# A decoder trunk on one core: the first four recurrent tiles with the tokens as the stationary side, turned by transfers, and the first gating batch behind another order of units

## The chip, the cores and the metric

One core of one Trainium2 chip runs the whole kernel. The metric is device time of one execution in microseconds. Three runs of the kernel before gave 965.71, 966.05 and 967.69, a median of 966.05 us. Beside these stands one profiled execution with its trace; every row quoted below is from it.

## The reference

A trunk of two layers over 256 tokens of width 1024, in float32. Layer 0 mixes tokens by a gated linear recurrence (RG-LRU), layer 1 by attention; around each mixer stand two half-step SwiGLU networks of width 2816, and every part is normalised before and after. The change touches the recurrent block only:

```python
def recurrent_block(x, w_in, conv_w, conv_b, w_a, b_a, w_x, b_x, lam, w_out):
    gx = x @ w_in
    gate, rec = gx[..., :D_RNN], gx[..., D_RNN:]
    rec = causal_depthwise_conv(rec, conv_w, conv_b)
    rec = rg_lru(rec, w_a, b_a, w_x, b_x, lam)
    return (jax.nn.gelu(gate) * rec) @ w_out
```

D_RNN is 1344. The convolution has four taps along the tokens. Inside rg_lru two small block-diagonal products (16 blocks of 84) with a sigmoid give the gates r and i; then log_a = -8 r softplus(-lam), a = exp(log_a), u = sqrt(1 - a^2) i x, and the state is h = a h + u along the tokens.

## The kernel before, in words

**Products.** Every operand is cut into a high and a low half: on the weights' side ACT copies the high half (whi, line 173) and DVE subtracts the low half (wlo, line 177). A product is three matmuls: high by high, low by high, high by low. `mm3` (lines 181 to 185) holds tokens still and streams weight columns; `mm3w` (lines 187 to 192) holds weights still and streams the 256 tokens.

**Units.** The program is a list of items, each with a `prep` (load on SP's queue into one of 5 raw buffers, then the split into one of 9 pairs of buffers) and a `work` (matmuls). `slot` runs one item for one half of the tokens (t = 0 or 1) or for both, then calls `tick`. `tick` counts down deferred steps (`defer(n, fn)` runs fn n ticks later), starts the next item's prep, and takes steps from a queue, each with a price, against a purse of 0.8 a tick. The order of TensorE's instructions is as written; ACT, DVE, POOL and SP are ordered by the framework, by when each step becomes possible and by what waits for it.

**The recurrent stage.** Its 1344 recurrent columns are eleven tiles of rows: ten of 126 and one of 84, in pairs p = 0 to 5. Units g0 to g10 make the gate branch, tokens still (g0 to g3 the first 504 columns, g4 to g7 the next 504, g8 to g10 the last 336; "0g5" is unit 5 for t = 0). Units r0 to r5 make the recurrent branch, weights still, so that the result has channels on the partitions and tokens along the row: 96 matmuls of 256 tokens for r0 and r1 together. `RG_ORDER` is the order of units, written by hand.

**From a pair to y.** After r_p, `conv` (lines 741 to 759) copies the pair out of its bank on ACT (line 748) and adds three taps a tile on DVE (line 754). Unit gw_p (line 761) multiplies it by the gate blocks into two banks (line 795), and ACT takes tanh of these (line 809). `after_gates` then has tanh and exp on ACT (line 828) and a chain on DVE (lines 829 to 838). For every two pairs stands a `batch` (line 845): a square root on ACT (line 853), the pending gelus of the gate branch (line 856), on DVE the products and the scan (lines 861, 862, 867), the gate branch turned by TensorE (line 877) or, for t = 0 of batches 0 and 1, by a transfer (`gate_turn`, line 694: POOL copies to 16-bit halves, an SP transfer transposes, POOL joins), the product y (line 886), its high half on ACT (line 887) and its low half on DVE (line 892). tanh, exp, square root and gelu need table loads on ACT where they follow one another. `w_out` (lines 183 to 185, reading y) takes tile k of y as its step k: steps 0 to 3 are batch 0, 4 to 7 batch 1, 8 to 10 batch 2. For t = 0 it runs eight steps, then six for t = 1, then the rest.

Of the kernel before, what the change touches and what calls it, by code (L numbers as in the profile page):

```python
# [43 lines left out]
def trunk_kernel(ctx: ExitStack, tc: tile.TileContext, A: dict, out: bass.AP):  # L44
# [13 lines left out]
    def nm(s):  # L58
        uid[0] += 1
        return f"{s}_{uid[0]}"  # L60
# [20 lines left out]
    def defer(n, fn):  # L81
        pend.append([n, fn])
# [73 lines left out]
    def load_raw(src, parts, n, pieces=1):  # L156
        v = new_raw()[:parts, :n]
        if len(src.shape) == 3:
            a, m = src.shape[1] // pieces, n // pieces
            for c in range(pieces):  # L160
                nc.sync.dma_start(v[:, c * m:(c + 1) * m].rearrange("p (a b) -> p a b", a=a),
                                  src[:, c * a:(c + 1) * a, :])
        else:
            nc.sync.dma_start(v, src)
        return v
# [52 lines left out]
    def join(dst, turned):  # L218

        nc.gpsimd.tensor_copy(dst, turned.rearrange("p (h f) -> p h f", h=2))  # L220
# [436 lines left out]
    def w_in(c0, n, k0, kn):  # L657
        return A["rg_w_in"][0, k0 * P:(k0 + kn) * P, c0:c0 + n].rearrange("(k p) n -> p k n", p=P)
# [6 lines left out]
    def add_gate_unit(g, k0, kn):  # L665
        c0, nn = GCOLS[g]

        def prep():
            return split(load_raw(w_in(c0, nn, k0, kn), P, kn * nn), P, kn * nn)

        def work(t, u):
            if k0 == 0:
                gacc[(g, t)] = mmbank()
            ps = gacc[(g, t)][:, :nn]
            for j in range(kn):
                k = k0 + j
                mm3(ps, *main_x(t, k), u.hi[:, j * nn:(j + 1) * nn], u.lo[:, j * nn:(j + 1) * nn], k == 0, k == 7)
            if k0 + kn == 8:

                if t not in toks:  # L680
                    toks[t] = pools["r"].tile([P, DRNN], F32, name=f"tok{t}")
                tok = toks[t][:, c0:c0 + nn]
                if t == 0 and g < 2:
                    nc.scalar.activation(tok, ps, AF.Gelu_apprx_tanh)
                    defer(5 - 3 * g, lambda: gate_turn(g))
                else:
                    nc.scalar.activation(tok, ps, AF.Copy)
                    plain.append(tok)
        rg[f"g{sum(n[0] == 'g' and n[1] != 'w' for n in rg)}"] = len(items)
        items.append((prep, work))  # L690
# [3 lines left out]
    def gate_turn(g):  # L694

        halves = hpool.tile([P, 512], F32, tag="t1", name=nm("pl"), bufs=2).bitcast(U16)
        hv = halves.rearrange("p (h j f) -> p h j f", h=2, j=4)
        src = toks[0][:, 4 * g * RT:4 * (g + 1) * RT].bitcast(U16)
        nc.gpsimd.memset(hv[:, :, :, RT:], 0)
        nc.gpsimd.tensor_copy(hv[:, :, :, :RT], src.rearrange("p (j f h) -> p h j f", h=2, f=RT))  # L700
        turned = pools["r"].tile([P, 512], F32, tag="turned", name=nm("turned"), bufs=1).bitcast(U16)
        out = tokT[g] = pools["r"].tile([P, 4, P], F32, tag="tokT", name=nm("tokT"), bufs=2)
        flat = out.rearrange("p a b -> p (a b)").bitcast(U16).rearrange("p (f h) -> p h f", h=2)
        defer(1, lambda: swap(turned, halves))
        defer(4, lambda: join(flat, turned))

    def tiles_of(p):
        return [2 * p, 2 * p + 1] if p < 5 else [10]
# [32 lines left out]
    def conv(p, ps):  # L741
        tl, w = tiles_of(p), pw(p)
        if p >= 4:
            flush(("y", (p - 4) // 2))
        xc = pools["r"].tile([RT, 2, S], F32, tag="xc", name=nm("xc"), bufs=4)
        xcs[p] = xc
        for j, i in enumerate(tl):
            nc.scalar.activation(xc[:w, j, :], ps[:w, j * S:(j + 1) * S], AF.Identity,
                                 bias=par[:w, 4 * NRT + i:4 * NRT + i + 1], scale=par[:w, 3 * NRT + i:3 * NRT + i + 1])

        def taps(j, i):
            for k in (2, 1, 0):
                s = 3 - k
                nc.vector.scalar_tensor_tensor(xc[:w, j, s:], ps[:w, j * S:(j + 1) * S - s],
                                               par[:w, k * NRT + i:k * NRT + i + 1], xc[:w, j, s:], ALU.mult, ALU.add)

        first = [(1.25, ("c", p), lambda j=j, i=i: taps(j, i)) for j, i in enumerate(tl)]
        n = max([i for i, q in enumerate(queue) if q[1][0] == "c"], default=-1)
        queue[n + 1:n + 1] = first
# [147 lines left out]
    def parts_of(g):  # L907
        return [(0, 4, RT)] if g < 2 else [(0, 2, RT), (2, 3, BLK)]

    for g in range(2):  # L910
        for k0 in range(0, 8, 2):
            add_gate_unit(g, k0, 2)
    for p in range(4):
        add_rec_units(p)
    for k0 in (0, 3, 6):
        add_gate_unit(2, k0, min(3, 8 - k0))
    add_rec_units(4)
# [1 line left out]
    for p in range(6):  # L919
        gw_unit(p)  # L920
    n_rg = len(items)
    RG_ORDER = ("0g0 0g1 0g2 0g3 0g4 0g5 0g6 0g7 1g0 1g1 r0 1g2 r1 gw0 1g3 1g4 r2 gw1 1g5 1g6 r3 gw2 1g7 "
                "0g8 0g9 0g10 r4 gw3 r5 1g8 gw4 1g9 1g10 gw5").split()
    OUT_ORDER = [0] * 8 + [1] * 6 + [0] * 3 + [1] * 5

    gbox = {}
# [543 lines left out]
```

## Time and profile before

| What | Value |
|---|---|
| median of 3 runs | 966.05 us |
| the profiled execution | 965.92 us |
| its span, first to last instruction | 964.2 us |
| outside the span | 1.7 us |
| granted TensorE clock over the span | 0.999 |
| TensorE busy | 955.9 us |
| DVE busy | 640.7 us |
| ACT busy | 527.6 us |
| POOL busy | 218.2 us |
| recurrent stage on TensorE, from first gate unit to w_out | about 190 to 268 us |

The profile is a page and a trace that answers questions: a timeline of one engine (start, length, engine, line, operation, tiles and shapes, how many were put together, and in brackets idle time before with its releaser), the chain of work that ended last, the waits by line, groups of equal instructions, and busy times by stretches. All times count from the start of the span. In a timeline, a row's length is that of the instruction with its latency; the next one on the engine can start before its end, so a run of instructions is added up from start to start.

### The profile page before, as it was taken

The page shows a single profiled execution, that of the slowest core. Times are in us where ns is not written, and L with a number is a line of the kernel's source. Part 1 is how long each engine was busy: PE and PEld are TensorE (multiplying, and loading weights), DVE is VectorE, ACT ScalarE, POOL GpSimd, SP SyncE. Part 2 cuts the span into 40 slices and gives each one's busy share as a digit, 9 for nine tenths or more (in the row PEclk, how much of TensorE's full clock was granted, in tenths as well). Part 3 has the DMA queues.
Part 4 walks back from the last instruction along what each step waited for, and adds up shares of the span by engine and source line. Part 5 has one row for each costly group of instructions (what it writes and reads, how often), then busy time and mean ns, then how long its engine had stood idle before and what let it go on. Part 6 is the DMA issues. An engine that isn't in the chain of part 4 may idle for free.

```text
span 964.2 us, 12866 instructions
## 1 busy us (share of the span) xinstructions
PE 955.9 (99%) x4575; PEld 791.3 (82%) x4575; DVE 640.7 (66%) x845; ACT 527.6 (55%) x750; POOL 218.2 (23%) x221
## 2 busy tenths in 40 slices
PE   9999999999999999999999999999999999999997
PEld 6888888898878888888898888888887788888886
DVE  6658674678997666664686566665488876666642
ACT  7546453568886555443565455444366855444431
POOL 2712330130001323230003522234022012232200
PEclk9999999999999999999999999999999999999999
DMA  8787995475346787775558979878773468777731
GB/s 286 226 258 225 256 284 197 142 228 163 119 123 219 209 236 211 205 242 196 135 182 278 253 219 258 230 216 265 226 256 97 133 199 236 207 222 233 223 109 44
DMA packets 148934, 198.79 MB, mean 206 GB/s; under 512 B 67166, under 2 KB 85958, under 8 KB 148742
## 3 DMA queue, kind: packets, MB, share of 16 engines
q1 hardware_dynamic: 146182, 191.06, 65.6%
q0 software_dynamic: 2080, 6.38, 2.1%
q8 instruction: 36, 0.59, 0.2%
q10 hardware_dynamic: 608, 0.53, 0.2%
q14 instruction: 28, 0.23, 0.1%
HBM read 182.19 MB, written 3.16 MB: 192 GB/s over the span
## 4 chain that ended last, share of the span: by engine, by line
PE 95%; DVE 2%; ACT 1%; issue 1%; POOL 0%; DMA 0%; POOLq 0%; DVEq 0%; ACTq 0%
PE mm L428 16%; PE mm L429 16%; PE mm L432 16%; PE mm L183 13%; PE mm L185 13%; PE mm L184 13%; PE gt L795 2%; PE mm L1305 1%; PE mm L190 1%; PE mm L191 1%; PE mm L192 1%; PE gt L226 1%; ACT pe L1181 1%; DVE wlo L177 0%; PE tr L127 0%
## 5 line engine op out<-in xcount | busy, mean ns | idle before, releaser
L177 DVE TENSOR_TENSOR wlo<-raw,whi 128x1024 fp32r<-128x1024 f32 (+5 forms) x329 | 418.0, 1276 | 230.7 <-ACT whi L173 228.3
L173 ACT ACTIVATE whi<-raw 128x1024 fp32r<-128x1024 f32 (+5 forms) x329 | 341.9, 1045 | 308.6 <-PE mm L432 119.2
L428 PE MATMUL mm<-whi,xhi 128*128 128x512 f32 x656 | 256.6, 391 | 0.0
L429 PE MATMUL mm<-wlo,xhi 128*128 128x512 f32 x656 | 255.5, 389 | 0.0
L432 PE MATMUL mm<-whi,xlo 128*128 128x512 f32 x656 | 202.1, 389 | 0.0
L428 PEld LDWEIGHTS mm<-whi,xhi 128*128 128x128 f32 x656 | 123.2, 188 | 25.9 <-issue 0.7
L432 PEld LDWEIGHTS mm<-whi,xlo 128*128 128x128 f32 x656 | 123.1, 188 | 25.8 <-DVE xlo L240 0.2
L429 PEld LDWEIGHTS mm<-wlo,xhi 128*128 128x128 f32 x656 | 123.2, 188 | 25.4 <-DVE wlo L177 0.3
L183 PE MATMUL mm<-whi,hhi 128*128 128x512 f32 x352 | 137.2, 390 | 0.0
L185 PE MATMUL mm<-whi,hlo 128*128 128x512 f32 x352 | 137.0, 389 | 0.0
L184 PE MATMUL mm<-wlo,hhi 128*128 128x512 f32 x352 | 136.9, 389 | 0.0
L540 POOL COPY pl<-prod 128x1024 uint16<-128x1024 uint16 (+1 forms) x48 | 69.9, 1456 | 174.4 <-DMA prod<-pl 174.4
L527 POOL COPY pl<-prod 128x1024 uint16<-128x1024 uint16 (+1 forms) x48 | 66.3, 1382 | 151.9 <-DVE prod L524 86.8
L183 PEld LDWEIGHTS mm<-whi,hhi 128*128 128x128 f32 x352 | 66.1, 188 | 13.7
L185 PEld LDWEIGHTS mm<-whi,hlo 128*128 128x128 f32 x352 | 66.1, 188 | 13.7
L184 PEld LDWEIGHTS mm<-wlo,hhi 128*128 128x128 f32 x352 | 66.1, 188 | 13.6
L198 POOL TENSOR_SCALAR nv<-ss 128x1 f32<-128x1 f32 x22 | 9.6, 437 | 268.7 <-ACT junk L205 268.7
L524 DVE SCALAR_TENSOR_TENSOR prod<-mm,rstd,sil 128x512 f32<-128x512 f32 (+1 forms) x48 | 33.8, 703 | 29.5 <-PE mm L432 25.9
L515 ACT ACTIVATE sil<-mm,rstd 128x512 f32<-128x512 f32 (+1 forms) x48 | 31.0, 649 | 32.9 <-PE mm L432 25.0
L546 DVE TENSOR_TENSOR hlo<-pl,hhi 128x512 fp32r<-128x512 f32 (+1 forms) x48 | 41.2, 858 | 3.7 <-ACT hhi L545 3.7
L183 PE MATMUL mm<-whi,xhi 128*128 128x512 f32 (+1 forms) x112 | 42.8, 382 | 0.0
L185 PE MATMUL mm<-whi,xlo 128*128 128x512 f32 (+1 forms) x112 | 42.5, 379 | 0.0
(223 smaller groups left out, 1054.6 us busy)
## 6 DMA issues: line engine op xcount, KB each, us to landing
raw<-in_ffn_w_down_dram SPq DMA_DIRECT2D x88, 512.0 KB
raw<-in_ffn_w_up_dram SPq DMA_DIRECT2D x80, 512.0 KB
raw<-in_ffn_w_gate_dram SPq DMA_DIRECT2D x78, 512.0 KB
raw<-in_rg_w_in_dram SPq DMA_DIRECT2D x10, 504.0 KB
raw<-in_rg_w_out_dram SPq DMA_DIRECT2D x10, 504.0 KB
raw<-in_ffn_w_gate_dram SPq DMA_DIRECT2D x19, 256.0 KB
raw<-in_ffn_w_up_dram SPq DMA_DIRECT2D x16, 256.0 KB
raw<-in_rg_w_in_dram SPq DMA_DIRECT2D x8, 512.0 KB
```

The costliest lines, as they stand in the source:

```text
L173: up = nc.scalar.activation(hi[:parts, c:c + m], rawv[:, c:c + m], AF.Copy)
L177: nc.vector.tensor_tensor(lo[:parts, c:c + m], rawv[:, c:c + m], hi[:parts, c:c + m].bitcast(F32), ALU.subtract)
L183: nc.tensor.matmul(ps, xh, wh, start=first, stop=False)
L184: nc.tensor.matmul(ps, xh, wl, start=False, stop=False)
L185: nc.tensor.matmul(ps, xl, wh, start=False, stop=last)
L428: nc.tensor.matmul(ps, get_x(t, k)[0], u.hi[:, c], start=k == 0, stop=False)
L429: nc.tensor.matmul(ps, get_x(t, k)[0], u.lo[:, c], start=False, stop=False)
L432: nc.tensor.matmul(ps, get_x(t, k)[1], u.hi[:, c], start=False, stop=k == nk - 1)
L524: nc.vector.scalar_tensor_tensor(pr[:, :nn], ps, rs[t][:, 0:1], s, ALU.mult, ALU.mult)
L527: nc.gpsimd.tensor_copy(halves.rearrange("p (h f) -> p h f", h=2), pr[:, :nn].bitcast(U16).rearrange("p (f h) -> p h f", h=2))
L540: nc.gpsimd.tensor_copy(halves.rearrange("p (f h) -> p h f", h=2), turned.rearrange("p (h a) b -> p h (a b)", h=2))
L546: keep(nc.vector.tensor_tensor(lv, x, hv.bitcast(F32), ALU.subtract))
```

## The change

Three things change.

1. r0 and r1 go. In their place a new kind of unit, `add_tok_unit` (R0 to R3, for t = 0 and 1), multiplies the first 504 recurrent columns with the tokens still: 6 matmuls of 504 columns a unit, 48 in all. After R3 the result has tokens on the partitions. ACT copies it (rtok), POOL copies it to 16-bit halves, an SP transfer transposes it, and POOL joins the halves into rT. The convs of pairs 0 and 1 come 7 and 8 ticks after 1R3 and read rT; their ACT copies are pinned in the order of the program.
2. `RG_ORDER` is a new one. gw0 stands after 0g7 and 1g4 stands behind it; r2 and 1g3 now stand ahead of gw0. From gw1 on TensorE's order of units is as it was, but for 1g6, which stands behind gw2 and no longer ahead of r3.
3. `gate_turn(0)` is deferred by 9 ticks, not by 5.

The functions behind keep their text and move in the file: lines 746 to 784 of before are 37 further down, 785 to 959 are 40 further down.

The framework's order on the other engines shifts with it. Four places follow. The names in the rows are: th gates, tt the batch's work tile, xc a conv's pair, y the batch's result, tok a gate tile, whi and wlo halves of a weight.

ACT at the first batch's square root (the 126x1024 row). Before:

```order
L748 ACTIVATE xc_2147<-mm_2098,par 126x256 x2
L809 ACTIVATE th_2166<-gt_2153,hb 126x256
L809 ACTIVATE th_2167<-gt_2153,hb 126x256
L809 ACTIVATE th_2166<-gt_2154,hb 126x256
L809 ACTIVATE th_2167<-gt_2154,hb 126x256
L828 ACTIVATE tt_2075<-th_2166,sp_101 126x256 x2
L828 ACTIVATE th_2166<-th_2166,sp_102 126x256 x2
L173 ACTIVATE whi_2348<-raw_2346 128x1008
L173 ACTIVATE whi_2392<-raw_2390 128x672
L853 ACT_TABLE_LOAD
L853 ACTIVATE tt_2075<-tt_2075 126x1024
```

and now:

```order
L868 ACT_TABLE_LOAD
L868 ACTIVATE th_2123<-th_2123,sp_102 126x256 x2
L849 ACTIVATE th_2166<-gt_2153,hb 126x256
L849 ACTIVATE th_2166<-gt_2154,hb 126x256
L849 ACTIVATE th_2167<-gt_2153,hb 126x256
L849 ACTIVATE th_2167<-gt_2154,hb 126x256
L173 ACTIVATE whi_2182<-raw_2180 128x1008
L868 ACTIVATE tt_2147<-th_2166,sp_101 126x256 x2
L868 ACTIVATE th_2166<-th_2166,sp_102 126x256 x2
L173 ACTIVATE whi_2282<-raw_2280 128x672
L893 ACT_TABLE_LOAD
L893 ACTIVATE tt_2147<-tt_2147 126x1024
```

Before, two pairs of conv copies and three weight splits lay between pair 0's and pair 1's gates; now pair 0's exp stands right ahead of pair 1's gates.

ACT in w_out, from y of batch 1 to the square roots of batch 2. Before:

```order
L887 ACTIVATE y_2588<-y_2587 126x512
L887 ACTIVATE y_2588<-y_2592 126x512
L828 ACTIVATE th_2533<-th_2533,sp_102 126x256
L809 ACTIVATE th_2606<-gt_2597,hb 84x256
L809 ACTIVATE th_2607<-gt_2597,hb 84x256
L828 ACTIVATE tt_2600<-th_2606,sp_101 84x256
L173 ACTIVATE whi_2645<-raw_2643 126x1024
L828 ACTIVATE th_2606<-th_2606,sp_102 84x256
L173 ACTIVATE whi_2661<-raw_2659 126x1024
L853 ACT_TABLE_LOAD
L853 ACTIVATE tt_2600<-tt_2600 126x512
L853 ACTIVATE tt_2600<-tt_2600 84x256
```

and now, from the second y row on:

```order
L927 ACTIVATE y_2561<-y_2565 126x512
L868 ACTIVATE tt_2589<-th_2500,sp_101 126x256
L868 ACT_TABLE_LOAD
L868 ACTIVATE th_2500<-th_2500,sp_102 126x256 x2
L173 ACTIVATE whi_2621<-raw_2619 126x1024
L868 ACTIVATE tt_2589<-th_2579,sp_101 84x256
L893 ACT_TABLE_LOAD
L893 ACTIVATE tt_2589<-tt_2589 126x512
L868 ACT_TABLE_LOAD
L868 ACTIVATE th_2579<-th_2579,sp_102 84x256
L173 ACTIVATE whi_2680<-raw_2678 126x1024
L893 ACT_TABLE_LOAD
```

Before, both square roots of batch 2 follow one table load. Now pair 4's root comes ahead of the exp of pair 5 (84 rows), whose root follows after two more table loads.

DVE at the products of batch 1. Before:

```order
L867 SCALAR_TENSOR_TENSOR tt_2418<-th_2278,tt_2418 126x256 x2
L867 SCALAR_TENSOR_TENSOR tt_2418<-th_2458,tt_2418 126x256 x2
L829 SCALAR_TENSOR_TENSOR xc_2436<-th_2534,xc_2436 126x512
L886 TENSOR_TENSOR y_2587<-tokT_1906,tt_2418 126x512
L886 TENSOR_TENSOR y_2592<-tr_2582,tt_2418 126x512
L892 TENSOR_TENSOR y_2589<-y_2587,y_2588 126x512
L892 TENSOR_TENSOR y_2589<-y_2592,y_2588 126x512
L833 TENSOR_SCALAR th_2533<-th_2533 126x512
L834 SCALAR_TENSOR_TENSOR th_2534<-tt_2600,th_2533 126x512
```

and now:

```order
L869 SCALAR_TENSOR_TENSOR xc_2409<-th_2501,xc_2409 126x512
L907 SCALAR_TENSOR_TENSOR tt_2447<-th_2425,tt_2447 126x256 x2
L177 TENSOR_TENSOR wlo_2576<-raw_2573,whi_2575 126x1024
L926 TENSOR_TENSOR y_2560<-tokT_2133,tt_2447 126x512
L926 TENSOR_TENSOR y_2565<-tr_2555,tt_2447 126x512
L177 TENSOR_TENSOR wlo_2586<-raw_2583,whi_2585 126x1024
L932 TENSOR_TENSOR y_2562<-y_2560,y_2561 126x512
L932 TENSOR_TENSOR y_2562<-y_2565,y_2561 126x512
L869 SCALAR_TENSOR_TENSOR xc_2467<-th_2580,xc_2467 84x256
```

Now one weight split stands between the last scan and the first product, and one between the second product and the lows.

ACT where the first conv stands, now:

```order
L687 ACTIVATE tok_1983<-mm_1939 128x512
L173 ACTIVATE whi_1988<-raw_1986 128x960
L173 ACTIVATE whi_2012<-raw_2010 128x960
L785 ACTIVATE xc_2028<-rT_1829,par 126x256 x2
L785 ACTIVATE xc_2047<-rT_1829,par 126x256 x2
L785 ACTIVATE xc_2065<-mm_1997,par 126x256 x2
L173 ACTIVATE whi_2070<-raw_2068 128x640
L684 ACTIVATE tok_1882<-mm_2074 128x512
```

The two convs that read rT stand behind the split of a gate weight, and r2's conv behind them.

The diff:

```diff
--- before.py
+++ after.py
@@ -682,7 +682,7 @@
                 tok = toks[t][:, c0:c0 + nn]
                 if t == 0 and g < 2:
                     nc.scalar.activation(tok, ps, AF.Gelu_apprx_tanh)
-                    defer(5 - 3 * g, lambda: gate_turn(g))
+                    defer(9 if g == 0 else 2, lambda: gate_turn(g))
                 else:
                     nc.scalar.activation(tok, ps, AF.Copy)
                     plain.append(tok)
@@ -703,6 +703,43 @@
         flat = out.rearrange("p a b -> p (a b)").bitcast(U16).rearrange("p (f h) -> p h f", h=2)
         defer(1, lambda: swap(turned, halves))
         defer(4, lambda: join(flat, turned))
+    racc, rtok = {}, {}
+    def add_tok_unit(k0, kn):
+        nn = 4 * RT
+        def prep():
+            return split(load_raw(w_in(DRNN, nn, k0, kn), P, kn * nn), P, kn * nn)
+        def work(t, u):
+            if k0 == 0:
+                racc[t] = mmbank()
+            ps = racc[t][:, :nn]
+            for j in range(kn):
+                k = k0 + j
+                mm3(ps, *main_x(t, k), u.hi[:, j * nn:(j + 1) * nn], u.lo[:, j * nn:(j + 1) * nn], k == 0, k == 7)
+            if k0 + kn == 8:
+                tok = pools["r"].tile([P, 4, P], F32, tag="y", name=nm("rtok"), bufs=2).rearrange("p a b -> p (a b)")
+                nc.scalar.activation(tok[:, :nn], ps, AF.Copy)
+                halves = pools["r"].tile([P, 2, S], F32, tag="xc", name=nm("pl"), bufs=4).rearrange("p a b -> p (a b)")
+                halves = halves.bitcast(U16)
+                hv = halves.rearrange("p (h j f) -> p h j f", h=2, j=4)
+                nc.gpsimd.memset(hv[:, :, :, RT:], 0)
+                nc.gpsimd.tensor_copy(hv[:, :, :, :RT],
+                                      tok[:, :nn].bitcast(U16).rearrange("p (j f h) -> p h j f", h=2, f=RT))
+                if t == 0:
+                    rtok["T"] = pools["r"].tile([P, 4, S], F32, tag="tt", name=nm("rT"), bufs=3)
+                turned = tok.bitcast(U16)
+                dst = rtok["T"][:, :, t * P:(t + 1) * P].bitcast(U16).rearrange("p a (b h) -> p h a b", h=2)
+                defer(1, lambda: swap(turned, halves))
+                defer(4, lambda: nc.gpsimd.tensor_copy(dst, turned.rearrange("p (h a b) -> p h a b", h=2, a=4)))
+                if t == 1:
+                    for p in range(2):
+                        defer(7 + p, lambda p=p: conv(p, rtok["T"][:, 2 * p:2 * p + 2, :].rearrange("p a b -> p (a b)")))
+        rg[f"R{k0 // 2}"] = len(items)
+        items.append((prep, work))
 
     def tiles_of(p):
         return [2 * p, 2 * p + 1] if p < 5 else [10]
@@ -745,8 +782,11 @@
         xc = pools["r"].tile([RT, 2, S], F32, tag="xc", name=nm("xc"), bufs=4)
         xcs[p] = xc
         for j, i in enumerate(tl):
-            nc.scalar.activation(xc[:w, j, :], ps[:w, j * S:(j + 1) * S], AF.Identity,
-                                 bias=par[:w, 4 * NRT + i:4 * NRT + i + 1], scale=par[:w, 3 * NRT + i:3 * NRT + i + 1])
+            last = nc.scalar.activation(xc[:w, j, :], ps[:w, j * S:(j + 1) * S], AF.Identity,
+                                        bias=par[:w, 4 * NRT + i:4 * NRT + i + 1],
+                                        scale=par[:w, 3 * NRT + i:3 * NRT + i + 1])
+            if p < 2:
+                tc.keep_in_program_order(last)
 
         def taps(j, i):
             for k in (2, 1, 0):
@@ -907,11 +947,14 @@
     def parts_of(g):
         return [(0, 4, RT)] if g < 2 else [(0, 2, RT), (2, 3, BLK)]
 
-    for g in range(2):
-        for k0 in range(0, 8, 2):
-            add_gate_unit(g, k0, 2)
-    for p in range(4):
-        add_rec_units(p)
+    for k0 in range(0, 8, 2):
+        add_tok_unit(k0, 2)
+    for k0 in range(0, 8, 2):
+        add_gate_unit(0, k0, 2)
+    add_rec_units(2)
+    for k0 in range(0, 8, 2):
+        add_gate_unit(1, k0, 2)
+    add_rec_units(3)
     for k0 in (0, 3, 6):
         add_gate_unit(2, k0, min(3, 8 - k0))
     add_rec_units(4)
@@ -919,8 +962,8 @@
     for p in range(6):
         gw_unit(p)
     n_rg = len(items)
-    RG_ORDER = ("0g0 0g1 0g2 0g3 0g4 0g5 0g6 0g7 1g0 1g1 r0 1g2 r1 gw0 1g3 1g4 r2 gw1 1g5 1g6 r3 gw2 1g7 "
-                "0g8 0g9 0g10 r4 gw3 r5 1g8 gw4 1g9 1g10 gw5").split()
+    RG_ORDER = ("0R0 0R1 0R2 0R3 0g0 0g1 0g2 0g3 1R0 1R1 1R2 1R3 1g0 1g1 1g2 1g3 r2 0g4 0g5 0g6 0g7 gw0 1g4 gw1 "
+                "1g5 r3 gw2 1g6 1g7 0g8 0g9 0g10 r4 gw3 r5 1g8 gw4 1g9 1g10 gw5").split()
     OUT_ORDER = [0] * 8 + [1] * 6 + [0] * 3 + [1] * 5
 
     gbox = {}
```

## The prediction

> **What bounds the kernel now.** I read the page first, for the busy shares and for the chain that ended last:
>
> ```profile
> PE 955.9 (99%) x4575; PEld 791.3 (82%) x4575; DVE 640.7 (66%) x845; ACT 527.6 (55%) x750; POOL 218.2 (23%) x221
> ...
> PE 95%; DVE 2%; ACT 1%; issue 1%; POOL 0%; DMA 0%; POOLq 0%; DVEq 0%; ACTq 0%
> ```
>
> TensorE is busy 99% of the span and is 95% of the chain, so time moves only if TensorE gets less to do, or if it is made to wait. Next the waits (engine, line, what it waited for: us in all, times, longest), in the window from 262 us on, where the recurrent stage ends and w_out runs:
>
> ```profile
> PE gt L795 <- issue: 0.8, 1, 0.8
> ...
> PEld mm L185 <- DVE y L892: 0.2, 1, 0.2
> ```
>
> These two are all that TensorE loses there: 0.84 us ahead of the last gate unit gw5, and 0.2 us where w_out wants the low half of the last y batch. Three more views, the timelines of TensorE, ScalarE and VectorE, give where each sits.
>
> **The change part by part.** First the matmuls. Stretches of TensorE (from:to, length, busy), and two steps of the chain in w_out:
>
> ```profile
> 204.29:209.91 5.62, 5.62 (x50) 1.00 0.28 58
> 216.92:219.80 2.88, 2.88 (x18) 1.00 0.51 140
> 222.67:228.29 5.62, 5.62 (x49) 1.00 0.03 10
> ...
> 268.71 0.23 PE mm L184
> 274.16 0.23 PE mm L184
> ```
>
> The first is pair r0: 48 matmuls of 256 columns in 5.62 us, 117 ns each. So r0 and r1, 96 matmuls, cost 11.24 us. In their place stand 48 of 504 columns. No row has 504; 24 steps of 512 columns lie between the last two lines: 5.45/24 = 0.227 us each. By columns 504 costs 0.2235, so 48 cost 10.73 to 10.90 (if a step doesn't shrink); at the 256-column price per column it would be 11.06. I take 10.8, the 512-column row being nearest: **-0.44** (ends -0.2 and -0.5). The transposing work around it lies on ACT, POOL and SP; see below.
>
> Second, gw0's place. The second line is gw0 at 216.92, the third r2. In the new order 1g3 and r2 stand ahead of gw0, which before came after it. 1g3 and 1g4 fill 219.80 to 222.67, so 1g3 is 1.43. gw0 moves by 1.43 + 5.62 - 0.44 = **+6.6**. gw1 keeps its predecessors and moves by -0.44, as does all after it that doesn't wait (but for r3 and gw2, 1.4 earlier still, since 1g6 now follows them).
>
> What gw0 needs is there in time. Pair 0 and 1 now go ACT copy, POOL halves, SP transpose, POOL join, conv. The nearest rows are those of the gate tiles:
>
> ```profile
> POOL tokT L220 <- DMA turned<-pl: 5.6, 2, 3.2
> ...
> 200.39 8.86 SPq L216 DMA_TRANSPOSE turned<-pl  x2
> ...
> 202.42 1.02 POOL L700 COPY pl<-tok 128x1008 uint16<-128x1008 uint16 x1 [2.00 <-ACT tok L684]
> 205.93 2.07 POOL L220 COPY tokT<-turned 128x1024 uint16<-128x1024 uint16 x1 [2.48 <-DMA turned<-pl]
> 211.16 2.36 POOL L220 COPY tokT<-turned 128x1024 uint16<-128x1024 uint16 x1 [3.16 <-DMA turned<-pl]
> ```
>
> The first transpose took 5.5 us (200.39 to the join at 205.93), the second some 3.1. So from the end of 1R3: copy 0.6, halves 1.0 to 1.5, transpose 3.1 to 5.5, join 2.4: 7.1 to 10.0 us. After 1R3 TensorE still does 1g0-3 (24 steps, 5.45), r2 (5.62) and 0g4-7 (5.45): 16.5 us. conv(0) stands on ACT behind a weight split that waits for the 34th of r2's matmuls, 9.4 us after 1R3, so the data lands about then; split, copies and taps (1.0, 0.5, then on DVE a split of 1.13 and six taps of 0.40) end at 14.5, gw0 starts at 16.5. No cost is taken; a transpose more than 2 us slower than the slow one would show.
>
> Third, the chain behind gw0. Batch 0's square root needs both pairs' gates. ACT before:
>
> ```profile
> 219.91 1.57 ACT L809 ACTIVATE th<-gt,hb 126x256 f32<-126x256 f32 x4 [0.95 <-PE gt L795]
> 221.35 0.62 ACT L828 ACTIVATE tt<-th,sp 126x256 f32<-126x256 f32 x1
> ...
> 222.96 1.28 ACT L828 ACT_TABLE_LOAD   x1
> 224.25 1.10 ACT L828 ACTIVATE th<-th,sp 126x256 f32<-126x256 f32 x2
> 225.25 2.52 ACT L173 ACTIVATE whi<-raw 128x960 fp32r<-128x960 f32 x3
> ...
> 232.72 1.10 ACT L828 ACTIVATE tt<-th,sp 126x256 f32<-126x256 f32 x2
> ...
> 234.68 1.70 ACT L173 ACTIVATE whi<-raw 128x1008 fp32r<-128x1008 f32 x2
> 236.40 1.28 ACT L853 ACT_TABLE_LOAD   x1
> 237.70 1.06 ACT L853 ACTIVATE tt<-tt 126x1024 f32<-126x1024 f32 x1
> ```
>
> In the new order ACT runs without a gap from gw0's first tanh, 219.91 + 6.6 = 226.5. From start to start in these rows: four tanh 1.44, one 0.49, a split 0.95, one 0.62, table load 1.29, two exp 1.00, gw1's four tanh 1.44, split 0.94, four more 1.96, split 0.78 (the last two splits are 234.68 to 236.40), table load 1.30. Sum 12.2: the square root starts at 238.7, not 237.70, **1.05 late**. gw1's gates, complete before 231, are no longer what it waits for.
>
> Fourth, what that lateness reaches. VectorE, and the two units that wait for it:
>
> ```profile
> 238.79:260.10 21.31, 21.13 (x36) 1.00 0.44 162
> ...
> 259.62 0.48 DVE L754 SCALAR_TENSOR_TENSOR xc<-mm,par,xc 126x253 f32<-126x253 f32 x1
> 260.64 0.69 DVE L834 SCALAR_TENSOR_TENSOR th<-tt,th 126x512 f32<-126x512 f32 x1
> ...
> 260.73 2.96 PE L795 MATMUL gt<-xc,gw 126*126 126x256 f32 x16
> 265.92 0.65 PE L877 MATMUL tr<-ident,tok 128*126 128x128 f32 x4
> 267.41 1.06 PE L795 MATMUL gt<-xc,gw 84*84 84x256 f32 x4 [0.84 <-issue]
> ...
> 262.85 1.06 ACT L853 ACTIVATE tt<-tt 126x1024 f32<-126x1024 f32 x1
> ```
>
> From batch 0's first step after the root (238.79) to pair 4's last tap (260.10) VectorE is busy 21.13 of 21.31 us. The new order holds the same instructions between these two, so nothing takes up the 1.05: the tap ends at 261.15. gw4 stands at 260.29 and its second matmul, 0.36 later, needs that tap: a new wait of about 0.55. It costs nothing by itself. gw5 waits for ACT to empty its banks behind two table loads; that ACT run starts from gw3 and moves by -0.44 (its root, 262.85, waits for L834, 261.33 + 1.05 = 262.4, the same moment). So gw5 starts at 267.41 - 0.44 = 266.97, the 0.84 shrinks to 0.3, and w_out begins 0.44 early.
>
> Fifth, y of batch 1 and 2. Before:
>
> ```profile
> 269.83 0.68 DVE L886 TENSOR_TENSOR y<-tokT,tt 126x512 f32<-126x512 f32 x1
> 270.43 0.68 DVE L886 TENSOR_TENSOR y<-tr,tt 126x512 f32<-126x512 f32 x1
> 271.81 1.29 DVE L892 TENSOR_TENSOR y<-y,y 126x512 fp32r<-126x512 f32 x2 [0.69 <-ACT y L887]
> ...
> 254.41 2.35 DVE L177 TENSOR_TENSOR wlo<-raw,whi 126x1024 fp32r<-126x1024 f32 x2
> ...
> 271.16 1.14 ACT L887 ACTIVATE y<-y 126x512 fp32r<-126x512 f32 x2
> 276.41 1.28 ACT L853 ACT_TABLE_LOAD   x1
> 277.70 0.99 ACT L853 ACTIVATE tt<-tt 126x512 f32<-126x512 f32 x2
> ...
> 274.23 0.39 PE L185 MATMUL mm<-whi,y 126*128 126x512 f32 x1
> ...
> 288.04 0.62 DVE L892 TENSOR_TENSOR y<-y,y 126x256 fp32r<-126x256 f32 x2
> 288.54 0.47 PE L185 MATMUL mm<-whi,y 126*128 126x512 f32 x1
> ```
>
> A weight split (two take 2.35, the first 1.22, so 1.13 from start to start) now stands ahead of the first product, and a second one ahead of the lows. The product starts at 269.83 + 1.05 + 1.13 = 272.0, ends 272.7; y's high half on ACT at 272.7, not 271.16: **+1.55** (before, ACT was 0.65 behind the product). The low is done at 272.6 + 0.6 + 1.13 + 0.7 = 275.0. The matmul that reads it came at 274.23, 1.7 after the first low's end (271.81 + 0.69); it now wants to come at 273.8: a new wait of **1.2**.
>
> From y's high half to the root of pair 4 ACT took 6.54 before (271.16 to 277.70). The new rows: y and tanh twice 2.16, load 1.29, two exp 1.0, split 0.95, tanh 0.6, load 1.29: 7.29, **+0.75**, since pair 4's exp moves behind with its load and pair 5's second part goes. Root at 280.0. From there to the low half VectorE took 10.34; the new rows, laid end to end with the same durations, take 10.2, **-0.1**: root 0.65, pair 4's chain 2.6, pair 5's three steps 1.1, splits 1.13, 1.12 and 1.13, pair 5's scan and the products 2.5. Two further table loads (pair 5 has its own exp and root) lie beside this with 0.8 us left. So the low of batch 2 is ready 1.55 + 0.75 - 0.1 = 2.2 late, 290.66. TensorE, at -0.44 + 1.2 - 0.2, comes at 289.1 and waits 1.6. Everything behind moves with it: a TensorE that is 99% busy has no gap to take it back.
>
> **Sum.** 288.46 (288.04 + 0.42) to 290.66: **+2.2 us** on the profiled execution's 965.92 is 968.1; the median of the runs lies 0.13 higher, so I say 968.2.
>
> A rule that bears on the table loads: in the Trainium skill, "ScalarE: Activation LUTs", section "What ACT_TABLE_LOAD costs", puts a switch at about 1283 ns for the load and some 1380 ns more of drain, and its section "Table sets: the hidden batching unit" asks to do all exps before all square roots, which this order no longer does for pairs 4 and 5. The trace agrees with the 1.283 but shows no drain: the load at 276.41 is followed by the root at 277.70. What a drain would make of the time is rival (e).
>
> **Rivals.** (a) Not slower: the lateness of batch 0 is not there, because ACT's run behind gw0 is shorter or pauses of VectorE take it up. Then the last low is 1.15 late and the time 967.1. It decides at 0.75 us of lateness, below which the total is under 0.2%. Against it: 0.18 us of pause in 21.31. For it: the lateness is one sum of 21 instructions, and a small difference of large numbers. (b) The new waits don't form at all: only -0.44 and the 0.2 are left, 965.3. It needs 2.2 us of error in one chain. (c) Slower: the transposes come late at gw0. SP is in order, and loads stand ahead of them. Past 2 us over the slowest seen, each us delays gw0 and all behind; 2 more give 970. (d) 504 columns cost as much as two of 256, so nothing is gained: ACT and VectorE's runs, which start from gw0 and gw3, are 0.44 later: 968.6. (e) Slower still: each table load stops ACT for its own length again, 1.28. The one more ahead of pair 4's root then costs 1.3 more, and the two beside VectorE 2.6 more, of which 0.8 is covered: 971. Against it: the root follows its load at once, 1.29 after its start.
>
> **How the numbers follow.** Forecast 0.51, (a) 0.21, (b) 0.05, (c) 0.07, (d) 0.10, (e) 0.02, and 0.04 for a gain that I don't see. The range 966.2 to 969.8 holds the forecast with its unknowns (lateness 0.6 to 1.5, matmuls -0.2 to -0.5, and as much again for what the rows don't show), (a) and (d), and leaves out the rest, 0.18. 0.2%, about what a measurement of this kernel can tell from no change, is 1.9 us: the border lies at 968.0, just under the forecast. Slower: 0.33 of the forecast, (c), (d) and (e): 0.52. Within: the forecast's other 0.18, (a) and (b): 0.44. Faster: 0.04.
>
> **What would show it.** r0 and r1's 11.24 us turned into 10.8; gw0 at about 223.5 with no wait; batch 0's root at 238.7; a wait of gw4 near 0.5 and gw5's below 0.5; w_out with waits for y's low half of about 1.2 and 1.6 us; four table loads on ACT between 272 and 285. If the first y wait is missing, the lateness of VectorE is wrong; if only the second is, the table loads are.

## The result, and the profile after

| | before | after |
|---|---|---|
| median of 11 runs | 965.70 us (965.65 to 967.90) | 968.32 us (967.94 to 969.04) |
| the profiled execution | 965.92 us | 968.32 us |
| its span | 964.2 us | 966.6 us |
| granted TensorE clock | 0.999 | 0.999 |
| after over before | | 1.0022, 95% interval 1.0014 to 1.0031 |

The change costs 0.22%, some 2.1 to 2.6 us; 968.2 was forecast. As a difference 2.6 was measured where 2.2 was forecast: the forecast started from a median of 966.05 in 3 runs, and 11 runs of the same kernel give 965.70.

Three slips in what stands ahead: the gate units have 512, 512 and 320 columns, and only the new units have 504. Between pair 0's and pair 1's gates ScalarE had one pair of conv copies and four weight splits before (225.25 to 230.3). And a tanh behind an exp or a gelu has no table load: the tanh of 232.25 in after follows the exp of 231.25 at once.

The page of after, busy shares and the chain that ended last:

```profile
PE 955.5 (99%) x4527; PEld 788.8 (82%) x4527; DVE 650.8 (67%) x845; ACT 531.6 (55%) x754; POOL 225.4 (23%) x227
...
PE 89%; DVE 4%; ACT 2%; issue 2%; DMA 1%; POOL 1%; POOLq 0%; DVEq 0%; ACTq 0%
```

TensorE's busy time hardly fell (955.9 before), and its share of the chain went from 95% to 89%: the path now leaves TensorE more often. In the recurrent stage the waits of TensorE from 262 to 300 us say where (us in all, times, longest):

```profile
PE mm L185 <- DVE y L932: 1.8, 2, 1.1
PE gt L835 <- issue: 0.6, 1, 0.6
```

Before, the only wait for y was one of 0.2 of the weight load (PEld). TensorE's timeline gives the places:

```profile
223.48 0.38 PE L835 MATMUL gt<-xc,gw 126*126 126x256 f32 x1
...
260.23 3.26 PE L835 MATMUL gt<-xc,gw 126*126 126x256 f32 x16
...
266.93 1.06 PE L835 MATMUL gt<-xc,gw 84*84 84x256 f32 x4 [0.61 <-issue]
...
273.52 0.39 PE L184 MATMUL mm<-wlo,y 126*128 126x512 f32 x1
274.55 0.50 PE L185 MATMUL mm<-whi,y 126*128 126x512 f32 x1 [0.65 <-DVE y L932]
...
288.79 0.39 PE L184 MATMUL mm<-wlo,y 126*128 126x512 f32 x1
290.28 0.50 PE L185 MATMUL mm<-whi,y 126*128 126x512 f32 x1 [1.10 <-DVE y L932]
```

From start to start a step is 0.23, so the two waits cost 1.03 - 0.23 = 0.80 and 1.49 - 0.23 = 1.26 us. ScalarE and VectorE in the same stretch:

```profile
238.66 1.06 ACT L893 ACTIVATE tt<-tt 126x1024 f32<-126x1024 f32 x1
...
272.20 0.63 ACT L927 ACTIVATE y<-y 126x512 fp32r<-126x512 f32 x1 [1.71 <-DVE y L926]
...
274.35 1.28 ACT L868 ACT_TABLE_LOAD   x1
...
278.20 1.28 ACT L893 ACT_TABLE_LOAD   x1
279.50 0.63 ACT L893 ACTIVATE tt<-tt 126x512 f32<-126x512 f32 x1
280.15 1.28 ACT L868 ACT_TABLE_LOAD   x1
...
283.01 1.28 ACT L893 ACT_TABLE_LOAD   x1
```

```profile
259.80 0.99 DVE L794 SCALAR_TENSOR_TENSOR xc<-mm,par,xc 126x254 f32<-126x254 f32 x2
...
270.37 1.20 DVE L177 TENSOR_TENSOR wlo<-raw,whi 126x1024 fp32r<-126x1024 f32 x1
271.48 0.68 DVE L926 TENSOR_TENSOR y<-tokT,tt 126x512 f32<-126x512 f32 x1
...
272.68 1.22 DVE L177 TENSOR_TENSOR wlo<-raw,whi 126x1024 fp32r<-126x1024 f32 x1
273.81 1.29 DVE L932 TENSOR_TENSOR y<-y,y 126x512 fp32r<-126x512 f32 x2
...
289.82 0.61 DVE L932 TENSOR_TENSOR y<-y,y 126x256 fp32r<-126x256 f32 x2
```

The batch-0 root stands 0.96 later than before (237.70), the two weight splits stand ahead of the product and of the low halves of y, there are four table loads, and the low half that TensorE waits for ends at some 290.24 where it ended at 288.46.

**A ruler for the experiments.** One profile can lie earlier or later as a whole. So each trace was lined up at a turn just ahead of the recurrent stage (line 330, the first turn of hn, 185.94 in before, 185.78 in after), and TensorE's lateness read at three places behind it: the start of w_out (268.12 before, 267.64 after), the second turn of h in the network behind (line 226, 304.36 and 306.12), and the last matmul (957.73 and 959.77). For after: 267.64 - 268.12 + 0.16 = -0.32 (-0.31 by the unrounded times), then +1.92 and +2.20. A plus is late. The last column is the time from the start of the last matmul to the end of the span.

| kernel | w_out | line 226 | last matmul | end | ratio to before (95%) |
|---|---|---|---|---|---|
| before, second profile | +0.01 | -0.01 | -0.05 | 6.48 | 1.0003 (0.9994 to 1.0011) |
| after | -0.31 | +1.92 | +2.20 | 6.85 | 1.0022 (1.0014 to 1.0031) |
| after, second profile | -0.31 | +1.91 | +1.94 | 6.85 | 1.0026 (1.0017 to 1.0035) |
| x1, old tiles, gw0 late | +0.02 | +0.95 | +0.95 | 6.48 | 1.0006 (0.9997 to 1.0015) |
| x2, y of batch 1 first | -0.31 | +2.04 | +2.07 | 6.85 | 1.0032 (1.0020 to 1.0045) |
| x8, roots together | -0.31 | +1.29 | +1.35 | 6.85 | 1.0016 (1.0008 to 1.0025) |
| x3, roots together and y priority | -0.31 | +0.66 | +0.71 | 6.86 | 1.0011 (1.0002 to 1.0019) |
| x4, x3 with x2 | -0.31 | +1.00 | +1.03 | 6.85 | 1.0014 (1.0005 to 1.0023) |
| x10, y priority alone | -0.31 | +2.69 | +3.02 | 6.86 | 1.0041 (1.0029 to 1.0054) |
| x5, ScalarE's order as before | -0.32 | -0.23 | +0.07 | 6.85 | 1.0003 (0.9994 to 1.0011) |
| x9, x5 with one gelu later | -0.67 | -0.24 | -0.17 | 6.86 | 1.0002 (0.9993 to 1.0011) |
| x7, gw0 one unit earlier | +0.40 | +3.11 | +3.41 | 6.87 | 1.0040 (1.0028 to 1.0053) |
| x12, x9 with six more DMAs | -0.67 | -0.22 | -0.22 | 6.48 | 1.0079 (1.0064 to 1.0093) |

### The profile page after: what moved, and what is told of

Same layout as the page of the kernel before. It is cut to its first block, busy times and chain, and to the rows that moved or that the text cites. A ratio compares the mean times of both kernels' runs of the same rounds, so it can differ in the third digit from the quotient of the medians.

```text
span 966.6 us, 12782 instructions
## 1 busy us (share of the span) xinstructions
PE 955.5 (99%) x4527; PEld 788.8 (82%) x4527; DVE 650.8 (67%) x845; ACT 531.6 (55%) x754; POOL 225.4 (23%) x227
## 4 chain that ended last, share of the span: by engine, by line
PE 89%; DVE 4%; ACT 2%; issue 2%; DMA 1%; POOL 1%; POOLq 0%; DVEq 0%; ACTq 0%
PE mm L428 16%; PE mm L429 16%; PE mm L432 16%; PE mm L185 12%; PE mm L183 12%; PE mm L184 12%; PE mm L1348 1%; DMA htok<-pl 1%; DVE wlo L177 1%; PE gt L226 1%; DVE tt L907 1%; DVE xc L794 1%; PE gt L1208 0%; PE mm L1251 0%; PE tr L127 0%
## 5 line engine op out<-in xcount | busy, mean ns | idle before, releaser
L177 DVE TENSOR_TENSOR wlo<-raw,whi 128x1024 fp32r<-128x1024 f32 (+4 forms) x329 | 425.6, 1300 | 226.5 <-ACT whi L173 224.5
L173 ACT ACTIVATE whi<-raw 128x1024 fp32r<-128x1024 f32 (+4 forms) x329 | 342.3, 1046 | 304.4 <-PE mm L432 132.1
L183 PE MATMUL mm<-whi,xhi 128*128 128x512 f32 (+2 forms) x128 | 49.1, 383 | 0.0
L185 PE MATMUL mm<-whi,xlo 128*128 128x512 f32 (+2 forms) x128 | 48.7, 381 | 0.0
L184 PE MATMUL mm<-wlo,xhi 128*128 128x512 f32 (+2 forms) x128 | 48.6, 380 | 0.0
```

What stands on the lines that cost most here:

```text
L173: up = nc.scalar.activation(hi[:parts, c:c + m], rawv[:, c:c + m], AF.Copy)
L177: nc.vector.tensor_tensor(lo[:parts, c:c + m], rawv[:, c:c + m], hi[:parts, c:c + m].bitcast(F32), ALU.subtract)
L183: nc.tensor.matmul(ps, xh, wh, start=first, stop=False)
L184: nc.tensor.matmul(ps, xh, wl, start=False, stop=False)
L185: nc.tensor.matmul(ps, xl, wh, start=False, stop=last)
```

## The experiments

**x1: what the late gating chain costs alone.** The kernel before, with gw0 (and pair 0's gates) behind r2, gw1 behind 1g5, and the old tiles kept.

```diff
-... r0 1g2 r1 gw0 1g3 1g4 r2 gw1 ...
+... r0 1g2 r1 1g3 1g4 r2 gw0 1g5 gw1 ...
```

> The kernel before, with r0 and r1 as they were (weights still, no transfers), and only gw0 moved behind r2 and gw1 behind 1g5. Theory (the late first gate unit and the tail behind it): gw0's first tanh at 228.4, batch 0's root at 239.7 instead of 237.7; half of that survives to y of batch 2, whose low half comes about 1.05 us late: the time is 1.0 to 1.3 us above before. Rival (the transposed tiles themselves cost the time, through POOL, ACT and transfers): nothing of them is here, so within 0.2 us of before.

Measured 966.80 us, and 0.95 on the ruler. TensorE's waits from 215 to 312 us are another set than in after, and one row of the weight load shows a wait for y:

```profile
PEld mm L185 <- DVE y L892: 0.5, 1, 0.5
PE gt L795 <- ACT whi L173: 0.5, 1, 0.5
...
PE mm L184 <- DVE wlo L177: 0.2, 1, 0.2
PE gt L795 <- issue: 0.2, 1, 0.2
```

The 0.95 forms behind the start of w_out. From start to start, the step that reads a weight's low half (277.38) and the one behind it take 0.48 more than usual, and the step that reads the low half of batch 2's y (289.71) and the one behind it 0.38 more. On the ruler that low half starts 0.95 late (289.25, and 288.04 before) and batch 0's root 1.85 (239.81).

So the lateness of gw0 alone does reach w_out, and costs about a microsecond in the trace (by the ratio of the runs 0.6, with an interval that reaches 0; 1.0 to 1.3 were expected). But the order at the roots stayed the old one: ScalarE still began pair 4's tanh and exp ahead of y, and both last roots follow one table load. So a late gw0 by itself doesn't bring the new order; which part of the change does was not isolated. The next runs price that order.

**x2, x8, x3, x4, x10: which part of that order.** All five are the changed kernel with some instructions held in program order or given priority.

x2 holds three low halves of weights on VectorE behind batch 1's y, whose products and low halves are held in program order too:

```diff
+            if pinned[0]:
+                pinned[0] -= 1
+                tc.keep_in_program_order(low)
```

> The changed kernel, with the two weight splits on DVE held behind y of batch 1. Theory: the first wait of w_out (0.8 us) goes, but one split on ACT falls between y and the tanh of pair 4, so batch 2's root is only 0.2 us earlier, TensorE arrives sooner and waits 2.1 us there: 0.2 us less than the changed kernel in all. If the first wait were worth its own length, 0.8 less. Rival (transposed tiles): no difference either, but both waits stay.

Measured 969.84 us; the expected 0.2 us less did not come. Its trace is 1.6 us late already ahead of the stage (and two of its five runs took 968.3 and 968.4), but on the ruler too nothing is won: 2.04, and 1.92 in after. TensorE's waits from 262 to 312:

```profile
PE mm L191 <- DVE y L940: 2.2, 1, 2.2
PE gt L841 <- issue: 0.6, 1, 0.6
```

The first wait is gone and the second has grown by it, to the 2.1 expected. The low half of batch 2 is ready at a time set by ScalarE and VectorE, whenever TensorE comes; of two waits in a row the last is the bound.

x8 holds pair 4's and 5's tanh and exp and the last square roots in program order, so that two table loads go:

```diff
+                    if p >= 4:
+                        tc.keep_in_program_order(a)
...
+                if g == 2:
+                    tc.keep_in_program_order(a)
```

> The changed kernel with pair 4's and 5's tanh and exp and the last two square roots in program order, so two table loads fewer, and no priority for y. If the table loads and the exp between the two roots make the second wait, this alone removes the wait of about 1.3 at 290 and gives 967.0, as with the priority; if the priority of y did it, the wait stays and the time is 968.0 to 968.3.

Measured 967.62 us, between the two: 0.63 of the 1.92 are gone, the second wait is 0.5.

x3 adds priority for the product and the low half of y of batches 1 and 2:

```diff
+            with tc.high_priority():
+                fn(t)
```

> The changed kernel, with tanh and exp of pairs 4 and 5 and both square roots of batch 2 pinned in the order of the program on ACT, and product and low half of batches 1 and 2 given priority. Two table loads less in w_out. Theory: the low half of batch 2 is ready at about 287, before TensorE wants it; the second wait (1.26 us) goes, the first stays: 1.2 to 1.3 us less than the changed kernel, about 967.0. Rival: the tail's order is not what costs, so 968.3 again.

Measured 966.94 us, as expected: the second wait is gone, only the first is left (0.6 in the view). ScalarE now reads:

```profile
274.44 1.28 ACT L868 ACT_TABLE_LOAD   x1
...
278.31 0.60 ACT L868 ACTIVATE th<-th,sp 84x256 f32<-84x256 f32 x1
278.93 1.28 ACT L896 ACT_TABLE_LOAD   x1
280.22 0.94 ACT L896 ACTIVATE tt<-tt 126x512 f32<-126x512 f32 x2
```

Pair 4's root is 0.7 later than in after (279.50), yet pair 5's follows at once, and not at 284.31.

x10 has the priority without the roots:

> The changed kernel with priority for the product and the low half of y of batches 1 and 2, and nothing else; the four table loads stay. Keeping the roots together took 0.65 us of 1.9 off TensorE's lateness at 320 us, both together 1.27. If the two shares add, this one takes 0.6 off and gives a second wait near 0.5: 967.4 to 967.7. If priority only helps behind an early root, it gives 968.0 to 968.3.

Measured 969.49 us, slower than after, outside both expectations. Its waits:

```profile
PE mm L183 <- ACT y L927: 1.1, 1, 1.1
PE mm L185 <- DVE y L932: 1.1, 2, 0.6
```

Priority put the lows of pair 4 on VectorE at 287.4, ahead of pair 5's last product and scan. The scan came at 289.58 (287.70 in after), so TensorE waited for pair 5's y instead. The two edits don't add: priority helps only if pair 5's root is early.

x4 is x3 with x2's pins:

> x2 and x3 together. Theory: both waits of w_out go, so the changed kernel is left with fewer matmul microseconds (0.3) and gw5's shorter wait: 2.1 to 2.6 us less than the changed kernel, 965.7 to 966.2, so level with before within 0.4. Rival: 968.

Measured 967.30 us; missed. y costs TensorE almost nothing now, but

```profile
PE mm L438 <- DVE xlo L246: 0.5, 1, 0.5
PE mm L191 <- DVE y L945: 0.2, 1, 0.2
```

VectorE is late for the next network's input (xlo): from 278 to 302 us it never stands idle for more than 0.15 at a time, so the splits that were pushed back are still ahead of it. A reorder of VectorE's work alone moves the wait on.

**x5: ScalarE's order put back.** The gelu of the last token tile is taken straight from PSUM, pair 4's tanh and exp are issued right behind it, ahead of y of batch 1; x3's edits stay. So x5 is not the order alone: it also spares ScalarE one copy of 320 columns (0.45 us in after, at 267.07) and has the priority for y.

```diff
+                    a = nc.scalar.activation(tok, ps, AF.Gelu_apprx_tanh)
+                    tc.keep_in_program_order(a)
+                    late.pop()()
```

> The changed kernel, with the order of ScalarE's work on pairs 4 and 5 put back to what it was before: the gelu of the last token tile is taken from PSUM directly, pair 4's two tanh and exp are issued right behind it and so ahead of y of batch 1, pair 5's exp and both last square roots stay together, and y of batches 1 and 2 has priority. Theory A (the 2.2 us come from the order of work at the roots of the last batch, which the later gw0 tipped over): TensorE waits for y nowhere, VectorE has pair 4's chain done before the root, the root comes near 278.8, and only the saved matmul time is left: 965.5 to 965.8, level with the kernel before or 0.3 under it. Theory B (the lateness of batch 0's square root, 1.0 us, reaches w_out whatever the order behind it): some 966.9, as in the run that only kept the roots together.

Measured 966.16 us beside 965.95 of before in the same session: level. From 262 to 300 us TensorE waits for y nowhere:

```profile
PE gt L840 <- issue: 0.6, 1, 0.6
```

ScalarE of x5: batch 0's root, then pair 4's tanh, table load and first exp ahead of y, where ScalarE now stands idle for 0.87 and not for 1.71 us as in after:

```profile
239.07 1.06 ACT L907 ACTIVATE tt<-tt 126x1024 f32<-126x1024 f32 x1
...
267.79 1.11 ACT L873 ACTIVATE tt<-th,sp 126x256 f32<-126x256 f32 x2
268.92 1.28 ACT L873 ACT_TABLE_LOAD   x1
270.21 0.60 ACT L873 ACTIVATE th<-th,sp 126x256 f32<-126x256 f32 x1
271.68 1.24 ACT L943 ACTIVATE y<-y 126x512 fp32r<-126x512 f32 x2 [0.87 <-DVE y L942]
...
278.12 1.28 ACT L907 ACT_TABLE_LOAD   x1
279.41 1.08 ACT L907 ACTIVATE tt<-tt 126x512 f32<-126x512 f32 x2
```

gw0 and batch 0's root are as late here as in after: on the ruler the root is 1.12 late in both. So theory B falls: with another order behind it, the same lateness costs TensorE nothing at w_out. VectorE's order followed ScalarE's: y's product starts at 270.96 with no split ahead of it, since the high half that this split needs now comes later on ScalarE. What x5's edits would give in the kernel before was not run, so they may also win back time that the lateness costs; the experiments don't divide after's 1.92 into lateness and order.

**x9: one gelu of 320 columns moved behind gw4's tanh.**

> The run that put ScalarE's order back (x5_act_as_before), and in it the gelu of the other 320-column tile moved from ahead of gw4's four tanh to behind them. gw5 waits 0.61 us until ScalarE has emptied its bank; the gelu takes 0.36 of ScalarE's time ahead of that. If gw5's wait is that of ScalarE's queue, it shrinks to 0.25, w_out begins 0.36 earlier, no new wait forms, and TensorE is 0.8 to 0.9 us ahead of the kernel before at 320 us (0.5 in x5_act_as_before): 965.2 to 965.8 for the whole. If the wait is for something else, it stays at 0.6 and so does the time.

Measured 966.08 us. gw5's wait shrank to 0.3 as expected and w_out began at -0.67, but at line 226 the lead is -0.24, as in x5:

```profile
PE mm L432 <- DVE xlo L240: 0.3, 1, 0.3
PE gt L840 <- issue: 0.3, 1, 0.3
```

What was won ahead of w_out is given back behind it to VectorE, as in x4. The 0.8 to 0.9 expected were thus wrong: x5's lead of 0.5 is that at the first turn of h, ahead of that wait, and behind it 0.23 is left.

**x7: how much cover the turned tiles have.** `0g6 0g7 gw0` became `0g6 gw0 0g7`.

> The changed kernel with gw0 one unit earlier, ahead of 0g7, so 1.36 us earlier in TensorE's order. If the turned tiles have the 2 us of cover that the prediction gave them, gw0 starts 1.36 earlier without a wait and the time falls or stays: 967.3 to 968.3. If they have only the 0.4 us that the trace of after shows (pair 0's last tap ends at 223.1, gw0 starts at 223.5), TensorE waits about 1.0 at gw0, the chain behind it is hardly earlier, and the time is 968.3 to 969.3.

Measured 969.49 us, slower than after by more than expected. gw0 stands idle ahead of its first matmul. The view names no releaser; the fifth of pair 0's six taps ends at 222.78 and the sixth at 223.18, so the taps are the likely reason, and not a shown one:

```profile
222.88 0.45 PE L835 MATMUL gt<-xc,gw 126*126 126x256 f32 x1 [0.41 <-issue]
```

So the cover is the small one, and gw0 one unit earlier costs at once, 0.7 us at w_out (0.40 and -0.31). That some 0.5 more is lost behind (3.11 against 1.92 on the ruler) was not taken apart.

**x6 and x11: the two kernels again,** for what differs outside the stage.

> The changed kernel itself, unchanged. It is there for the 1.13 us that TensorE waited at 750.9 for qT in the profile of after and for the output's 0.35. If these belong to the kernel, the profile shows them again and the time is 968.3; if they were of that one execution, TensorE's wait for qT is 0.3 as in the other runs, the span is 0.3 to 0.6 shorter, and the time is 967.8 to 968.0.

> The kernel before, unchanged, for the two places outside the stage where the profiles of one and the same changed kernel differ: the first 14 us (a shift of up to 1.9 us) and TensorE's wait for qT near 750 (0.3 or 0.9 to 1.1). If both are of the execution and not of the change, a second profile of before can show them too, and TensorE's times between 190 and 320 us differ from the first profile by one constant shift, within 0.1 us. The ratio should be 1.000.

x6: 968.07 us, x11: 965.92 us. From the stage on, TensorE in x11 is before with a shift of 0.02 to 0.07. x6 is after with a shift of 1.9 (187.69 in place of 185.78 ahead of the stage) that arises in the first 14 us, at the first loads, and it is the same on the ruler at line 226 (+1.91). TensorE's wait of 0.9 for qT near 750 us did not come back; 0.3 is left, as in before. GpSimd in the two traces of the one kernel, after first:

```profile
748.59 2.28 POOL L220 COPY qT<-htok 128x1024 uint16<-128x1024 uint16 x1 [4.55 <-DMA htok<-pl]
```

```profile
749.12 1.37 POOL L220 COPY qT<-htok 128x1024 uint16<-128x1024 uint16 x1 [3.17 <-DMA htok<-pl]
```

GpSimd waited 1.4 us longer for the transfer and the copy took 0.9 longer in one of them; after it TensorE is 0.26 later to the end (2.20 - 1.94). The same long wait stood in x5, x7 and x10 and in no other profile. In these traces it comes and goes in one and the same kernel; both profiles of before lack it, too few to say that it can't come there.

**x12: the end of the program.** Six more DMAs (three gate blocks loaded in halves) on x9.

> The run x9_gelu_later with six more DMAs: three gate weight blocks are loaded in two halves each, for both gates. It is there for the end of the program. In every profile of a kernel with the two added transposes the span ends 6.85 us after the start of the last matmul, with the old tiles 6.48. SyncE at the end waits for the DMA semaphores one after the other at some 0.06 us each; the output's are the 7th to 9th in the old kernels and come early in the changed ones, and the six others stand behind the last landing. DMAs take eight semaphores in turn, so two more DMAs turn the list, and eight more bring it back. If this is so, the end is 6.48 again and the time 965.6 to 965.8, level with the kernel before or 0.2 under it; if the 0.37 us have another cause, the end stays at 6.85 and the time is 966.0 to 966.2.

The end is 6.48 us again, as in before: what TensorE is ahead at its last matmul, 0.22, it still is at the end of the span. In the trace SyncE waits for the DMA semaphores one by one, 0.06 us each; in after six of them stand behind the last landing and the waits end at 5.98 us after the last matmul's start, in before and x12 they stand ahead of it and the waits end at 5.61. So 0.37 us of the loss are there, in every kernel with the two added transfers, and have nothing to do with the work of the recurrent stage. The time itself missed: 973.53 us. With the six DMAs TensorE waits in the first network, where x9 has no wait:

```profile
PE mm L183 <- DVE prod L524: 2.2, 1, 2.2
PE mm L428 <- ACT whi L173: 1.2, 1, 1.2
PE mm L429 <- DVE wlo L177: 0.8, 1, 0.8
```

The trace is 8.2 us late before the stage begins. The waits are 4.2 of it. Behind them, from 112 to 114 us and from 132 to 135, the granted clock is 0.50 (1.00 in x9) and a step takes 0.43 us in place of 0.23. That is an estimated 3 us more: the mean clock is 0.65 from 112 to 116 and 0.59 from 132 to 136, which loses 1.4 and 1.6 us. A wait alone doesn't do it: behind x2's of the same 2.2 us the clock stays at 1.00. How six small loads bring on the waits was not followed up.

## Why the prediction was right, step by step

The total was met within 0.2 us, and so were the places of both waits; the terms of the sum were off, and two costs outside the stage were not seen. That the total fits this well is in part luck (point 6).

The trace of after lies 0.16 us early ahead of the stage. The lateness of each place below is therefore given on the ruler: the time in after, less that in before, plus 0.16.

1. **Matmuls, -0.44 forecast, -0.26 measured.** By columns 504 should have cost less than 512. Two stretches of after, 24 steps of 504 columns (1R0 to 1R3) and 24 of 512 (from:to, length, busy and matmuls, granted clock, share and GB/s of the DMAs):

```profile
201.40:206.89 5.49, 5.49 (x25) 1.00 0.88 155
206.89:212.38 5.49, 5.49 (x25) 1.00 0.75 209
```

   Both are 0.229 a step, so 48 cost 10.98, not 10.8, in place of 11.24. The forecast and rival (d), that nothing is gained, lie on either side of it.

2. **Place and cover of gw0.** It stands at 223.48 (223.5 forecast) and does not wait. But the cover was 0.4 us and not 2: pair 0's last tap ends at 223.1, 1.7 later than worked out. Some 1.1 of this is one split of 960 columns on VectorE, which took 2.25 us in place of 1.16, beside a copy on GpSimd that had begun just before; the rest stands ahead of it, where ScalarE's half of this split (217.44) waited 0.52 for its weights:

```profile
216.95 1.16 DVE L177 TENSOR_TENSOR wlo<-raw,whi 128x960 fp32r<-128x960 f32 x1 [1.06 <-ACT whi L173]
218.48 2.25 DVE L177 TENSOR_TENSOR wlo<-raw,whi 128x960 fp32r<-128x960 f32 x1 [0.37 <-ACT whi L173]
```

```profile
218.42 1.36 POOL L220 COPY tokT<-turned 128x1024 uint16<-128x1024 uint16 x1 [3.52 <-DMA turned<-pl]
```

   x7 shows what the rest of the cover was worth.

3. **Batch 0's root, 1.05 late forecast, 1.12 measured** (238.66). The sum over the 21 instructions holds.

4. **Its reach.** VectorE's run to the last tap of pair 4 took 21.04 us in place of 21.31, so of 1.12 only 0.85 arrive (the tap ends at 260.79), where 1.05 was forecast. gw4 took 3.19 where it took 2.88, a wait of 0.31 for 0.55; it is its third matmul that waits (260.89), not the second. gw5 starts at 266.93 (266.97).

5. **y.** The high half stands at 272.20, 1.20 late, where 1.55 were forecast: 0.20 of the difference stand already at the tap, the rest between it and the product. From there to the root ScalarE took 7.30 (7.29), from the root to the low half 10.3 (10.2). The waits are 0.80 and 1.26 for 1.2 and 1.6, all four table loads are there, the low half of batch 2 is 1.94 late and TensorE behind the stage 1.92, where 2.2 were forecast. There is no sign of rival (e), a load that stops ScalarE for its own length again: the root of 279.50 starts 1.30 after its load, as before.

6. **What filled the gap.** 1.92 at line 226, 0.28 behind the wait for qT and 0.37 at the end, less the 0.16 by which the trace lies early, make 2.41, and the spans differ by 2.4. Costs that were not seen took the place of one set too high: the mechanism in the stage is right and its size 0.3 too large, and that the total came out so close is luck. The 0.28 is not in every profile of the changed kernel, the 0.37 is.

The reasons hold as mechanisms, with one addition from the experiments. The forecast added the lateness (1.05) to the price of the new order as if each were fixed. The runs show that what the lateness costs hangs on the order behind it: x5, with the same late root, waits for y nowhere, and x1, with the old order and a root 1.85 late, loses 0.95, not half of it to y.

## What to carry to other kernels

Where a change makes a chain late on engines whose order the framework sets by readiness, list what each of them now does first, and price that apart from the lateness: here the same late root stood behind 1.92 us with one order and nothing with another. Of several waits on the same chain only the last is the bound, and a reorder of a busy engine passes the wait on (x2, x4, x9). Before a saving below 0.5% is believed, take two profiles of each kernel and line them up ahead of the change: here first loads moved a trace by 1.9 us, and a cost that belongs to the end of the program was 0.37.

## What the runs showed that was not expected

- A matmul step of 504 columns costs as much as one of 512, 0.229 us (24 in 5.49 us each; in w_out before, 24 of 512 took 5.45).
- VectorE's splits of weights take about 1.2 us alone; in after seven of them, from 198 to 232 us, took 2.03 to 2.29, and each began while a copy on GpSimd was running. Where the split began first, it kept its 1.21 and the copy took longer. Before, for one:

```profile
205.57 1.21 DVE L177 TENSOR_TENSOR wlo<-raw,whi 128x1008 fp32r<-128x1008 f32 x1 [0.16 <-ACT whi L173]
```

  with the join of 205.93 at 2.07 us, in place of 1.36. The Trainium skill, "Trainium Architecture — The Big Picture", section "What this means for kernel authors", says that VectorE and GpSimd contend for one shared pair of ports and that it is an exclusive lock, not a split of bandwidth. These rows agree: the later one pays, by most of the overlap (1.09 us for one of 1.30 at 218.48, 0.71 for one of 0.85 at 205.93).
- The order in which SyncE waits for the DMA semaphores at the end turns with the number of DMAs and is worth 0.37 us.
- Six more DMAs among the program's loads cost 7.7 us at another place (x12, 973.53 beside 965.85), an estimated 3 of it through a granted clock of 0.50 behind two waits.
